# Part of a projection's row sums moved from TensorE to VectorE in the first stage of a transformer block

## The chip, the cores and the metric

The kernel runs on one core of a Trainium2 chip. The metric is the device time of one execution in microseconds (us). All data are float32 in memory. Engines: TensorE (PE; PEld is its weight load), VectorE (DVE), ScalarE (ACT), GpSimd (POOL), and SyncE (SP), which issues most of the transfers (DMA).

## The reference, cut to what matters

The whole block computes a modulated norm, two attention branches, a gated projection, and a feed-forward part with a convolution. The change touches only the first lines:

```python
c_act = jax.nn.silu(c)                       # 1 x 1024
mod = c_act @ w_ada[l] + b_ada[l]            # 1 x 6144
sh_m, sc_m, gt_m, sh_f, sc_f, gt_f = jnp.split(mod, 6, axis=-1)
h = modulate(rms_norm(x, g_mix[l]), sh_m, sc_m)   # 256 x 1024
proj = jnp.einsum('bsd,de->bse', h, w_in[l])      # its first 1536 columns: qa, ka, va
```

Feature `d` of `h` needs `sh_m[d]` and `sc_m[d]`, so it needs column `d` and column `1024 + d` of `c_act @ w_ada`: sums over 1024 rows.

## The kernel before, in words

The first stage works through the 1024 features in eight tiles `j` of 128. For each tile it loads `ada{j}` (two 1024 x 128 column strips of `w_ada`, laid out as 128 partitions x 2 x 8 row blocks x 128) and `wA{j}` (128 rows of `w_in`, 1536 columns). `row_sums(j)` forms the 256 column sums: for each of the eight row blocks `k` one product with the stationary operand `cw[:, k, :]`, which is 32 columns wide and holds `c` in column 0 and zeros elsewhere. Block `k` goes to the column group `k % 4` of the array, so two blocks are accumulated in each of the four groups of one PSUM bank, `cs`. VectorE copies `cs` to `row` (line 460). `column_sums(j)` (line 466) adds up the partitions of `row` and turns the sums into columns, `h`. From those ScalarE makes the scale and shift `ab` (lines 507 and 508) and the modulated features in rounded form, `hh` (line 509); VectorE makes the remainder `hl` (lines 514 and 515).

A product with a weight is formed from three: `hh` with the rounded weight `wh`, `hl` with `wh`, and `hh` with the weight's remainder `wl`. For the weight rows of a tile, `wh` comes from ScalarE in two pieces, `whA` and `whB` (line 553), and `wl` from VectorE in two, `wlA` and `wlB` (line 556). `products(j)` are the 30 products of tile `j`: 24 into the accumulators `pA` (line 472) and six into `pV` (line 477).

The order in this stage is written by hand, and each engine runs its list from front to back. In the loop over `j`, TensorE runs the first `M1[j]` products of tile `j` (9, 7, 5, and then 4), the row sums of tile `j + 1`, nine more products of tile `j`, the column sums of tile `j + 1`, and then the rest of tile `j`. VectorE runs, for tile `j + 1`: `row`, `wlA`, `hf` and `hl`, `wlB`. The loads of `wA{j+3}` and `ada{j+4}` follow at the end of an iteration. There are four buffers for `ada`, three for the raw weights.

After tile 7 come the gate projections (`ps_ga`, line 329) and the rest of the block, with TensorE busy almost without a break.

Of the kernel before, what the change touches and what calls it, by code (L numbers as in the profile page):

```python
# [9 lines left out]
F32 = mybir.dt.float32  # L10
F32R = mybir.dt.float32r
AF = mybir.ActivationFunctionType
ALU = mybir.AluOpType
# [4 lines left out]
P = 128  # L18
D = 1024
KT = D // P  # L20
S = 256
# [32 lines left out]
def block_kernel(ctx: ExitStack, tc: tile.TileContext, x, c, w_ada, b_ada, g_mix, w_in, w_br_moba,  # L54
                 w_br_sb, w_out, rel_bias, g_ffn, w_up, w_conv, b_conv, w_down, g_final, out):
    nc = tc.nc
# [5 lines left out]
    start = ExitStack()  # L62
    start.enter_context(tc.manual_schedule())
    const = ctx.enter_context(tc.tile_pool(name="const", bufs=1))
# [4 lines left out]
    small = ctx.enter_context(tc.tile_pool(name="small", bufs=2))  # L69
# [9 lines left out]
    def bank(pool, name):  # L79
        return pool.tile([P, 512], F32, tag="bank", name=name)  # L80
# [21 lines left out]
    ca = const.tile([P, KT], F32, name="ca")  # L102
# [9 lines left out]
    cw = const.tile([P, KT, 32], F32, name="cw")  # L112
    nc.vector.memset(cw, 0.0)
    nc.vector.tensor_copy(cw[:, :, 0], ca)


    warm = bank(sm, "warm")
# [228 lines left out]
    def tick():  # L346
        for task in list(tasks):
            task[0] -= 1
            if task[0] < 0:
                try:  # L350
                    task[0] = (next(task[1]) or 1) - 1
                except StopIteration:
                    tasks.remove(task)
# [70 lines left out]
    def bias_load():  # L424
        nc.sync.dma_start(toep, bass.AP(tensor=rdram.tensor, offset=rdram.offset,
                                          ap=[[1, P], [512, NH], [1, S]]))
# [11 lines left out]
    ads, wws = {}, {}  # L438

    def ada_load(j):  # L440

        ads[j] = st.tile([P, 2, KT, P], F32, tag="ada", name=f"ada{j}", bufs=4)
        for i in range(2):
            c0 = i * D + j * P
            nc.sync.dma_start(ads[j][:, i, :, :], w_ada[:, c0:c0 + P].rearrange("(k p) f -> p k f", p=P))

    def win_load(j):
        wws[j] = raw_tile(f"wA{j}")
        nc.sync.dma_start(wws[j][:, :1536], w_in[j * P:(j + 1) * P, QA:QA + 1536])  # L449

    def row_sums(j):


        cs = bank(sm, f"cs_{j}")
        for k in range(KT):
            g = slice(k % 4 * 32, k % 4 * 32 + 32)
            nc.tensor.matmul(cs[g, 0:S].rearrange("p (i f) -> p i f", i=2), cw[:, k, :], ads[j][:, :, k, :],  # L457
                             start=k < 4, stop=k >= 4)
        row = small.tile([P, S], F32, tag="acc0", name=f"row_{j}")
        nc.vector.tensor_copy(row, cs[:, 0:S])  # L460
        return row

    def column_sums(j, row):
        ps = bank(sm, f"h1_{j}")
        for i in range(2):
            nc.tensor.matmul(ps[:, i:i + 1], row[:, i * P:(i + 1) * P], ones[:, 0:1], start=i == 0, stop=i == 1)
        return ps

    def products(j, wp):

        def qk(n, f):
            nc.tensor.matmul(psqk[f // 2][:, f % 2 * S:(f % 2 + 1) * S], wp[0][n == 2][:, f * P:(f + 1) * P],  # L472
                             (hh, hl, hh)[n][:, j, :], start=j == 0 and n == 0 and f % 2 == 0,
                             stop=j == KT - 1 and n == 2 and f % 2 == 1)

        def v(n, t):
            nc.tensor.matmul(psv[t], (hh, hl, hh)[n][:, j, t * P:(t + 1) * P], wp[1][n == 2][:, 0:512],  # L477
                             start=j == 0 and n == 0, stop=j == KT - 1 and n == 2)

        if j == KT - 1:  # L480
            for b in (0, 2, 1, 3):
                for n in range(3):
                    for f in (2 * b, 2 * b + 1):
                        qk(n, f)
                        yield
            for t in range(NT):
                for n in range(3):
                    v(n, t)
                    yield
            return  # L490
        for n in range(3):
            for f in range(KT):
                qk(n, f)
                yield
            for t in range(NT):
                v(n, t)
                yield

    def run(gen, n=None):
        while n is None or n > 0:  # L500
            if next(gen, gen) is gen:
                return
            n = None if n is None else n - 1

    def modulated(j, ps):
        ab = small.tile([P, 2], F32, tag="ab", name=f"ab_{j}")
        nc.scalar.activation(ab[:, 0:1], ps[:, 1:2], AF.Identity, bias=bg[:, j:j + 1], scale=gmix[:, j:j + 1])
        nc.scalar.activation(ab[:, 1:2], ps[:, 0:1], AF.Identity, bias=vc[:, j:j + 1])
        nc.scalar.activation(hh[:, j, :], xT[:, j, :], AF.Identity, bias=ab[:, 1:2], scale=ab[:, 0:1])
        return ab  # L510

    def h_lo(j, ab):
        hf = small.tile([P, 512], F32, tag="hf", name=f"hf_{j}", bufs=3)[:, :S]
        nc.vector.tensor_scalar(hf, xT[:, j, :], ab[:, 0:1], ab[:, 1:2], op0=ALU.mult, op1=ALU.add)
        nc.vector.tensor_sub(hl[:, j, :], hf, hh[:, j, :].bitcast(F32))
# [22 lines left out]
    bg = const.tile([P, KT], F32, name="bg")  # L538
    nc.vector.tensor_mul(bg, b1[:, 8:16], gmix)
    row = row_sums(0)  # L540
    warm_up(4)
    put_xT(1, xt[1], nc.vector.tensor_copy)
# [3 lines left out]
    def w_parts(j):  # L546


        wh = [whp.tile([P, 1024], F32R, tag="wh", name=f"wh{x_}{j}") for x_ in "AB"]
        wl = [wlp.tile([P, 1024], F32R, tag="wl", name=f"wl{x_}{j}") for x_ in "AB"]  # L550

        def hi(i, a, n):
            nc.scalar.copy(wh[i][:, a:a + n], wws[j][:, i * 1024 + a:i * 1024 + a + n])  # L553

        def lo(i, a, n):
            nc.vector.tensor_sub(wl[i][:, a:a + n], wws[j][:, i * 1024 + a:i * 1024 + a + n],  # L556
                                 wh[i][:, a:a + n].bitcast(F32))

        return list(zip(wh, wl)), hi, lo
# [13 lines left out]
    for j in range(KT):  # L573
        todo = products(j, wp)
        if j + 1 < KT:
            wp, hi, lo = w_parts(j + 1)
            run(todo, M1[j])
            row = row_sums(j + 1)
            run(todo, M2)
            hi(0, 0, 1024)  # L580
            ab = modulated(j + 1, column_sums(j + 1, row))
            hi(1, 0, 512)
            lo(0, 0, 1024)
            h_lo(j + 1, ab)
            lo(1, 0, 512)
        run(todo)
        if j + 3 < KT:
            win_load(j + 3)
        if j + 4 < KT:
            ada_load(j + 4)  # L590
        if j == 4:
            bias_load()
        if j == 3:
            nc.scalar.copy(onesr, ones)
            nc.scalar.copy(tri, trif)
        tick()
# [581 lines left out]
```

## Time and profile before

| | us |
|---|---|
| median of three runs (lowest, highest) | 420.02 (418.63, 420.79) |
| the profiled execution's own time | 418.87 |
| its span, first to last instruction | 417.1 |
| TensorE busy / VectorE busy in the span | 402.3 / 315.8 |
| ScalarE busy / GpSimd busy in the span | 253.9 / 25.9 |

The profile is one execution. A row of a timeline gives the start and the length in us, engine, source line, operation, what is written from what, and how many instructions were merged into the row; brackets give the idle time before it and what ended that. On TensorE the length of a row includes the pipeline's end, so the start of the next row says when the engine went on. A row of the chain of waits gives start and length of a piece of the work that ended last.

### The profile page before, as it was taken

The page shows a single profiled execution, that of the slowest core. Times are in us where ns is not written, and L with a number is a line of the kernel's source. Part 1 is how long each engine was busy: PE and PEld are TensorE (multiplying, and loading weights), DVE is VectorE, ACT ScalarE, POOL GpSimd, SP SyncE. Part 2 cuts the span into 40 slices and gives each one's busy share as a digit, 9 for nine tenths or more (in the row PEclk, how much of TensorE's full clock was granted, in tenths as well). Part 3 has the DMA queues.
Part 4 walks back from the last instruction along what each step waited for, and adds up shares of the span by engine and source line. Part 5 has one row for each costly group of instructions (what it writes and reads, how often), then busy time and mean ns, then how long its engine had stood idle before and what let it go on. Part 6 is the DMA issues. An engine that isn't in the chain of part 4 may idle for free.

```text
span 417.1 us, 7453 instructions
## 1 busy us (share of the span) xinstructions
PE 402.3 (96%) x2956; PEld 369.1 (88%) x2956; DVE 315.8 (76%) x474; ACT 253.9 (61%) x405; POOL 25.9 (6%) x64
## 2 busy tenths in 40 slices
PE   7999999999999999999979999999999999999992
PEld 6778899999999999999857999999999998888881
DVE  3645579788578979999597899999978888546433
ACT  4544477787697897816375658666766676343412
POOL 4500000000000110000330000000000000000000
PEclk9999999999999999999999999999999999999997
DMA  8999998977556875876957686877566555564002
GB/s 272 335 327 332 341 323 272 334 253 258 198 179 229 262 281 173 281 239 224 321 167 240 211 263 215 264 243 250 166 212 182 202 170 170 176 242 133 21 0 101
DMA packets 75082, 94.49 MB, mean 227 GB/s; under 512 B 2573, under 2 KB 61072, under 8 KB 75047
## 3 DMA queue, kind: packets, MB, share of 16 engines
q1 hardware_dynamic: 74135, 91.82, 68.2%
q10 hardware_dynamic: 576, 1.57, 1.0%
q0 software_dynamic: 336, 0.62, 0.4%
q8 instruction: 23, 0.38, 0.4%
q14 instruction: 12, 0.10, 0.1%
HBM read 92.94 MB, written 1.06 MB: 225 GB/s over the span
## 4 chain that ended last, share of the span: by engine, by line
PE 88%; SPq 3%; DMA 3%; DVE 3%; issue 1%; ACT 1%; POOL 0%; POOLq 0%; ACTq 0%
PE ps_up L298 27%; PE ps_down L185 15%; PE ps_ga L329 6%; PE ps_gb L329 6%; PE pA L472 4%; PE ps_out L185 4%; PE ps_vb L329 3%; PE ps_qb L329 3%; PE ps_yb L329 3%; PE ps_kb L329 3%; PE ps_ya L329 3%; DMA ada<-in_w_ada_dram 2%; PE ps_up L185 2%; PE pV L477 2%; SPq L449 2%; PE cs L457 1%
## 5 line engine op out<-in xcount | busy, mean ns | idle before, releaser
L143 ACT CAST wh_up<-raw_up 128x1024 fp32r<-128x1024 f32 x44 | 46.1, 1049 | 26.6 <-PE ps_up L298 21.5
L298 PE MATMUL ps_up<-h2h__2633,wh_up 128*128 128x256 f32 x320 | 57.7, 282 | 0.0
L298 PE MATMUL ps_up<-h2h__2633,wl_up 128*128 128x256 f32 x320 | 57.4, 281 | 0.0
L298 PE MATMUL ps_up<-h2l__2634,wh_up 128*128 128x256 f32 x320 | 57.4, 281 | 0.0
L148 DVE TENSOR_TENSOR wl_up<-raw_up,wh_up 128x1024 fp32r<-128x1024 f32 x42 | 50.9, 1220 | 7.0 <-ACT wh_up L143 6.9
L298 PEld LDWEIGHTS ps_up<-h2h__2633,wh_up 128*128 128x128 f32 x320 | 46.4, 188 | 0.2
L298 PEld LDWEIGHTS ps_up<-h2h__2633,wl_up 128*128 128x128 f32 x320 | 46.3, 188 | 0.0
L298 PEld LDWEIGHTS ps_up<-h2l__2634,wh_up 128*128 128x128 f32 x320 | 46.3, 188 | 0.0
L148 DVE TENSOR_TENSOR wl_down<-raw_down,wh_down 128x1024 fp32r<-128x1024 f32 x22 | 26.9, 1224 | 25.5 <-ACT wh_down L143 25.5
L143 ACT CAST wh_down<-raw_down 128x1024 fp32r<-128x1024 f32 x22 | 23.1, 1052 | 32.1 <-PE ps_down L185 23.6
L1040 DVE SCALAR_TENSOR_TENSOR cv<-ps_up,wc,cv 128x255 f32<-128x255 f32 (+1 forms) x80 | 34.6, 477 | 1.4 <-ACT cv L1034 0.8
L185 PE MATMUL ps_down<-wh_down,hl_a 128*128 128x512 f32 x88 | 34.8, 395 | 0.0
L185 PE MATMUL ps_down<-wl_down,hh_a 128*128 128x512 f32 x88 | 34.8, 395 | 0.0
L185 PE MATMUL ps_down<-wh_down,hh_a 128*128 128x512 f32 x88 | 34.8, 395 | 0.0
L1034 ACT ACTIVATE cv<-ps_up,vc,wc 128x256 f32<-128x256 f32 x40 | 20.4, 561 | 5.9 <-PE ps_up L298 5.9
L553 ACT CAST whA<-raw_wA 128x1024 fp32r<-128x1024 f32 (+1 forms) x9 | 8.6, 952 | 21.3 <-DMA raw_wA<-in_w_in_dram 21.3
L185 PEld LDWEIGHTS ps_down<-wh_down,hl_a 128*128 128x128 f32 x88 | 16.5, 188 | 4.0
L185 PEld LDWEIGHTS ps_down<-wh_down,hh_a 128*128 128x128 f32 x88 | 16.6, 188 | 3.9
L185 PEld LDWEIGHTS ps_down<-wl_down,hh_a 128*128 128x128 f32 x88 | 16.5, 188 | 3.9
L556 DVE TENSOR_TENSOR wlA<-raw_wA,whA 128x1024 fp32r<-128x1024 f32 x8 | 9.8, 1226 | 8.5 <-ACT whA L553 8.4
L329 PE MATMUL ps_gb<-hh,wh_gb 128*128 128x256 f32 x64 | 13.2, 288 | 0.0
L329 PE MATMUL ps_ga<-hh,wh_ga 128*128 128x256 f32 x64 | 13.2, 288 | 0.0
(280 smaller groups left out, 968.6 us busy)
## 6 DMA issues: line engine op xcount, KB each, us to landing
raw_up<-in_w_up_dram SPq DMA_DIRECT2D x44, 512.0 KB, 5.3
raw_down<-in_w_down_dram SPq DMA_DIRECT2D x10, 1024.0 KB, 4.9
ada<-in_w_ada_dram SPq DMA_DIRECT2D x16, 512.0 KB, 8.1
raw_wA<-in_w_in_dram SPq DMA_DIRECT2D x8, 768.0 KB, 9.4
raw_ga<-in_w_in_dram SPq DMA_DIRECT2D x4, 1024.0 KB, 9.8
ada_gtm<-in_w_ada_dram SPq DMA_DIRECT2D x8, 512.0 KB, 5.4
ada_shf<-in_w_ada_dram SPq DMA_DIRECT2D x8, 512.0 KB, 5.0
raw_gb<-in_w_in_dram SPq DMA_DIRECT2D x4, 1024.0 KB
```

What stands on the lines that cost most here:

```text
L143: nc.scalar.copy(wh, t[:, a:a + 1024])
L148: eng.tensor_sub(wl, t[:, a:a + 1024], wh.bitcast(F32))
L185: nc.tensor.matmul(ps, sx(k)[:, sl], w[:, c0:c0 + n], start=first and i == 0, stop=last and i == 2)
L298: nc.tensor.matmul(st.ps[f // 2][:, f % 2 * S:(f % 2 + 1) * S], wi[:, kk * 512 + f * P:kk * 512 + (f + 1) * P], sx(k0 + kk), start=first a ...
L329: nc.tensor.matmul(st.ps[:, f * S:(f + 1) * S], cols[:, a] if st.fm else x_[:, a], x_ if st.fm else cols, start=first and kk == n == f == ...
L449: nc.sync.dma_start(wws[j][:, :1536], w_in[j * P:(j + 1) * P, QA:QA + 1536])
L472: nc.tensor.matmul(psqk[f // 2][:, f % 2 * S:(f % 2 + 1) * S], wp[0][n == 2][:, f * P:(f + 1) * P], (hh, hl, hh)[n][:, j, :], start=j == 0 ...
L477: nc.tensor.matmul(psv[t], (hh, hl, hh)[n][:, j, t * P:(t + 1) * P], wp[1][n == 2][:, 0:512], start=j == 0 and n == 0, stop=j == KT - 1 an ...
L553: nc.scalar.copy(wh[i][:, a:a + n], wws[j][:, i * 1024 + a:i * 1024 + a + n])
L556: nc.vector.tensor_sub(wl[i][:, a:a + n], wws[j][:, i * 1024 + a:i * 1024 + a + n], wh[i][:, a:a + n].bitcast(F32))
L1034: nc.scalar.activation(ct[:, b, :], tp[:, b * S:(b + 1) * S], AF.Identity, bias=bconv[:, fb:fb + 1], scale=wc[:, 88 + fb:89 + fb])
L1040: nc.vector.scalar_tensor_tensor(ct[:, b, d:], tp[:, b * S:(b + 1) * S - d], wc[:, (2 - d) * 44 + fb:(2 - d) * 44 + fb + 1], ct[:, b, d:], ...
```

## The change

For feature tiles 4 to 7, row blocks 3 to 7 of the weighted sum are formed on VectorE: one operation multiplies block 3 by `c`, and four more each multiply a block by `c` and add it to the sum so far, `csum`. They are in VectorE's list right after `wlB` of the tile before, one iteration ahead of the row sums that use them. TensorE then forms four products instead of eight: blocks 0, 1 and 2 as before, and `csum` with `ow`, which holds a one in column 0 and zeros elsewhere. Each of the four goes to its own column group. Tiles 0 to 3 are as before.

```diff
+    ow = const.tile([P, 32], F32, name="ow")
+    nc.vector.memset(ow, 0.0)
+    nc.vector.memset(ow[:, 0:1], 1.0)
+    sums = {}
...
         cs = bank(sm, f"cs_{j}")
-        for k in range(KT):
+        ops = [(cw[:, k, :], ads[j][:, :, k, :]) for k in range(KT)]
+        if j in sums:
+            ops[3:] = [(ow, sums[j])]
+        for k, (c_, a_) in enumerate(ops):
             g = slice(k % 4 * 32, k % 4 * 32 + 32)
-            nc.tensor.matmul(cs[g, 0:S].rearrange("p (i f) -> p i f", i=2), cw[:, k, :], ads[j][:, :, k, :],
-                             start=k < 4, stop=k >= 4)
+            nc.tensor.matmul(cs[g, 0:S].rearrange("p (i f) -> p i f", i=2), c_, a_, start=k < 4,
+                             stop=k + 4 >= len(ops))
...
+    def sum_rows(j):
+
+        sums[j] = (small.tile([P, 512], F32, tag="hf", name=f"csum_{j}", bufs=3)[:, 0:S]
+                   .rearrange("p (i f) -> p i f", i=2))
+        for k in range(3, KT):
+            if k == 3:
+                nc.vector.tensor_scalar(sums[j], ads[j][:, :, k, :], ca[:, k:k + 1], None, op0=ALU.mult)
+            else:
+                nc.vector.scalar_tensor_tensor(sums[j], ads[j][:, :, k, :], ca[:, k:k + 1], sums[j], op0=ALU.mult,
+                                               op1=ALU.add)
+            yield
...
             lo(1, 0, 512)
+            if 4 <= j + 2 < KT:
+                run(sum_rows(j + 2))
         run(todo)
```

In VectorE's list before, around the row copy of tile 4 (`row_501`; `wlB_423` belongs to tile 3, `wlA_486` to tile 4):

```order
L514 TENSOR_SCALAR hf_459<-xT,ab_453 128x256 [waits Activation_49]
L515 TENSOR_TENSOR hl<-hf_459,hh 128x256 [waits DVE_49,Activation_49]
L556 TENSOR_TENSOR wlB_423<-raw_wA_351,whB_357 128x512 [waits Activation_49]
L460 COPY row_501<-cs_492 128x256 [waits PE_49]
L556 TENSOR_TENSOR wlA_486<-raw_wA_415,whA_484 128x1024 [waits DMAHW5_49,Activation_49]
```

The same place in VectorE's list now (`row_506` is the row copy of tile 4, `csum_466` its partial sum):

```order
L533 TENSOR_SCALAR hf_462<-xT,ab_456 128x256 [waits Activation_49]
L534 TENSOR_TENSOR hl<-hf_462,hh 128x256 [waits DVE_49,Activation_49]
L575 TENSOR_TENSOR wlB_426<-raw_wA_354,whB_424 128x512 [waits Activation_49]
L476 TENSOR_SCALAR csum_466<-ada_356,ca 128x256 [waits DMAHW4_49,DMAHW3_49]
L478 SCALAR_TENSOR_TENSOR csum_466<-ada_356,ca,csum_466 128x256 [waits DVE_49] x4
L467 COPY row_506<-cs_501 128x256 [waits PE_49]
L575 TENSOR_TENSOR wlA_495<-raw_wA_418,whA_493 128x1024 [waits DMAHW5_49,Activation_49]
```

Five operations stand between `wlB` of tile 3 and the row copy of tile 4; the first waits for the load of `ada4`, each of the other four for the one ahead of it.

In TensorE's list before, around the row sums of tile 4 (`cs_492`), with the first products of tile 3 ahead of them:

```order
L472 MATMUL pA_267<-hh,whA_420 128x256 [waits Activation_49]
L472 MATMUL pA_267<-hh,whA_420 128x256
L472 MATMUL pA_268<-hh,whA_420 128x256 x2
L457 MATMUL cs_492<-ada_353,cw 32x256 [waits DMAHW4_49,DMAHW3_49,PE_49]
L457 MATMUL cs_492<-ada_353,cw 32x256 x7
L472 MATMUL pA_269<-hh,whA_420 128x256 x2
```

The same place in TensorE's list now (`cs_501` are the row sums of tile 4):

```order
L491 MATMUL pA_270<-hh,whA_423 128x256 [waits Activation_49]
L491 MATMUL pA_270<-hh,whA_423 128x256
L491 MATMUL pA_271<-hh,whA_423 128x256 x2
L464 MATMUL cs_501<-ada_356,cw 32x256 [waits DMAHW4_49,DMAHW3_49,PE_49]
L464 MATMUL cs_501<-ada_356,cw 32x256 x2
L464 MATMUL cs_501<-csum_466,ow 32x256 [waits DVE_49]
L491 MATMUL pA_272<-hh,whA_423 128x256 x2
```

The row sums stand where they stood, after four products of tile 3. Four of the eight are gone, and the last one left waits for VectorE.

## Rows read from the trace of the kernel before

**Rows 1.** The page's first part: busy us (share of span) and instructions of each engine.

```profile
PE 402.3 (96%) x2956; PEld 369.1 (88%) x2956; DVE 315.8 (76%) x474; ACT 253.9 (61%) x405; POOL 25.9 (6%) x64
```

**Rows 2.** The chain of waits, around and after the stage: start us, us, what.

```profile
17.59 9.49 DMA ada<-in_w_ada_dram
27.22 1.07 PE cs L457 x16
...
58.91 1.40 PE pV L477 x6
60.31 4.37 PE ps_ga L329 x36
```

**Rows 3.** Windows, one tile: PE, PEld, DVE, ACT, POOL busy; clock, DMA, GB/s.

```profile
38.00:43.88 5.88, 5.88 (x51) 4.90 (x51) 3.27 (x6) 2.67 (x5) 0.55 (x1) 1.00 1.13 330
```

**Rows 4.** Timeline of TensorE: row sums of tile 4; products and column sums of tile 5.

```profile
32.97 1.07 PE L457 MATMUL cs<-ada,cw 128*32 128x256 f32 x16
...
39.85 0.75 PE L472 MATMUL pA<-hh,whA 128*128 128x256 f32 x4
...
41.24 0.50 PE L466 MATMUL h<-ones,row 128*128 128x1 f32 x4
```

**Rows 5.** Short timelines of TensorE inside the row sums of tile 6.

```profile
44.72 0.42 PE L457 MATMUL cs<-ada,cw 128*32 128x256 f32 x4
44.96 0.61 PE L457 MATMUL cs<-ada,cw 128*32 128x256 f32 x8
45.17 0.61 PE L457 MATMUL cs<-ada,cw 128*32 128x256 f32 x8
45.39 0.40 PE L457 MATMUL cs<-ada,cw 128*32 128x256 f32 x4
45.72 0.39 PE L472 MATMUL pA<-hh,whA 128*128 128x256 f32 x1
```

**Rows 6.** Timeline of VectorE: end of tile 3; tile 5 to the next row copy.

```profile
32.24 0.69 DVE L556 TENSOR_TENSOR wlB<-raw_wA,whB 128x512 fp32r<-128x512 f32 x1
...
42.32 0.41 DVE L514 TENSOR_SCALAR hf<-xT,ab 128x256 f32<-128x256 f32 x1
...
43.46 0.69 DVE L556 TENSOR_TENSOR wlB<-raw_wA,whB 128x512 fp32r<-128x512 f32 x1
45.86 0.42 DVE L460 COPY row<-cs 128x256 f32<-128x256 f32 x1 [1.70 <-PE cs L457]
```

**Rows 7.** Timeline of ScalarE, tile 5.

```profile
41.78 0.35 ACT L507 ACTIVATE ab<-h,bg,vc 128x1 f32<-128x1 f32 x1 [0.65 <-PE h L466]
...
42.32 0.60 ACT L509 ACTIVATE hh<-xT,ab 128x256 fp32r<-128x256 f32 x1
```

**Rows 8.** VectorE's multiply-and-adds: durations by line (min/median/max ns), and one run.

```profile
L1040 DVE SCALAR_TENSOR_TENSOR cv<-ps_up,wc,cv x80: 466/475/486, 244.2 to 351.9; 128x255 f32<-128x255 f32 x40, 128x254 f32<-128x254 f32 x40
L839 DVE SCALAR_TENSOR_TENSOR acc_gtm<-ada_gtm,ca,acc_gtm x8: 1275/1280/1285, 71.0 to 104.8; 128x1024 f32<-128x1024 f32 x8
279.78 2.81 DVE L1040 SCALAR_TENSOR_TENSOR cv<-ps_up,wc,cv 128x255 f32<-128x255 f32 x7
```

**Rows 9.** Timeline of VectorE at the start.

```profile
3.86 0.27 DVE L113 MEMSET cw<- 128x256 f32 x1
4.17 0.17 DVE L114 COPY cw<-ca 128x8 f32<-128x8 f32 x1
5.41 0.15 DVE L133 TENSOR_SCALAR ms_n<-ss 128x1 f32<-128x1 f32 x1 [1.07 <-ACT sq L390]
```

**Rows 10.** Waits, one of TensorE: us in total, times, longest us.

```profile
PE ps_up L185 <- ACT h2h__2633 L153: 2.3, 1, 2.3
```

**Rows 11.** Windows, the stretch that holds this wait; columns as in rows 3.

```profile
206.00:228.00 22.00, 18.84 (x88) 14.26 (x87) 17.41 (x30) 13.51 (x25) 7.05 (x5) 1.00 0.63 198
```

**Rows 12.** One load of ada for tile 5: issue times, and us to landing.

```profile
L445 SPq DMA_DIRECT2D ada<-in_w_ada_dram x1: 1630/1630/1630, 29.4 to 29.4; - x1
DMA to landing us min/median/max: 8.7/8.7/8.7
```

## Prediction

> **What bounds the kernel now.** I read the page's busy times first. TensorE is busy for 96% of the span, VectorE for 76% [rows 1], so anything taken from TensorE counts if nothing else is made late. Then the chain of waits. Until 27 us it runs through transfers: the load of tile 3's `ada` is the last thing waited for, and from the row sums behind it the chain stays on TensorE, through tiles 3 to 7 and on into the gate projections [rows 2]. Tiles 4 to 7 are thus the part of the stage that TensorE alone sets. The windows, cut from tile to tile, show it: in the 5.88 us of one tile TensorE is busy for all of it, VectorE for 3.27 [rows 3]. Read as a share, VectorE has 2.6 us free per tile, and the added work would seem to fit. Whether it does hangs on where that free time lies, which only the timelines tell. VectorE idles for 1.70 us just ahead of the row copy [rows 6], and that idle time ends with the row sums, so most of it falls after the moment at which TensorE begins them. Work put there is free only if nobody asks for its result before the row sums are over. The last of the new row sums does ask.
>
> **What is removed.** The sixteen instructions of one tile's row sums (two for each float32 product) start in four rounds of four, at 44.72, 44.96, 45.17 and 45.39, and the next product begins at 45.72 [rows 5]: 1.00 us in all, each round some 0.22, the last 0.33 up to the next product. Two products per column group take four rounds, so one per group takes two. Without any wait a tile's row sums would last 0.57 us in place of 1.00. That saves 0.43 us a tile, and over four tiles 1.7 us.
>
> **What is added.** Five VectorE operations per tile on 256 columns. The trace has no such operation on `ada`; the nearest are the multiply-and-add on 255 columns, 0.475 us, and `hf`, a multiply on 256 columns, 0.41 us [rows 6, 8]. From below, seven such multiply-and-adds in one run took 2.81 us, one every 0.39, so they overlap a little; five in that rhythm end 2.04 us after the first starts. But those lie interleaved with operations on other tiles, while the new ones form a chain in which each waits for the one ahead. For such a wait the nearest row is `cw`: a fill of 0.27 us at 3.86, and the copy into it begins at 4.17, 0.04 after its end [rows 9]. With that, the chain takes 0.41 + 0.04 + 3 x (0.475 + 0.04) + 0.475 = 2.47 us. From above I allow 0.69 us each, what `wlB` costs on twice the columns [rows 6]: 3.45. I take 2.47, since it is built from rows of nearly the same size.
>
> The Trainium skill ("VectorE: DVE Perf Modes", section "The DRAIN you can't avoid") says that a semaphore behind each of a run of chained operations costs nothing over a single one at the end. By it the chain would take 2.04 us and not 2.47; the `cw` row speaks mildly against it, and what it would make of the time stands among the rivals.
>
> **Where the chain lies: the first tile.** VectorE starts `wlB` of tile 3 at 32.24, for 0.69 us [rows 6]; the next operation can start about 0.08 before its end (the overlap of the run of seven), at 32.85. The load it needs is there, since TensorE began the same tile's row sums at 32.97 with no idle time before them [rows 4]. So TensorE arrives when the chain has just begun. It ends at 35.32. I add 0.04 for the hand-over and then the last product: its two instructions sit in one column group and take two rounds, 0.22 + 0.33 = 0.55. TensorE goes on at 35.91, where before it went on at 32.97 + 1.00 = 33.97. Loss: 1.94 us, the saving of that tile included. Everything behind stands in the same queue: the other 26 products of tile 3, the column sums of tile 4, and so all of tile 4.
>
> **The three tiles after it.** A late start alone would move everything once. But the next chain hangs on this one through a loop. From the moment at which TensorE goes on after the row sums (39.85 for tile 5 in the trace): nine products up to the column sums at 41.24, so 1.39 [rows 4]; `ab` at 41.78, 0.54 later, having waited for TensorE; `hh` and `hf` at 42.32, another 0.54 [rows 6, 7]; `wlB` at 43.46, 1.14 later; the chain could start at 44.07, 0.61 later. Up to here 4.22 us. Then 2.47 for the chain, 0.04, and 0.55 for the last product: 7.28 us. TensorE's own round in the kernel before is 5.87, from 39.85 to 45.72 [rows 4, 5]. VectorE and TensorE now wait for each other in turn, and each of tiles 5, 6 and 7 takes 1.41 us longer: 4.23. The loads don't add to this: the second load of tile 5's `ada`, issued at 29.4, lands 8.7 later at 38.1 [rows 12], and the chain for tile 5 can't begin before 35.91 + 4.22 = 40.1.
>
> **The small parts.** The two fills of `ow` fall into the 1.07 us for which VectorE waits for ScalarE near the start [rows 9]; uncovered they would cost no more than `cw`'s 0.27 each. The load queue issues the same transfers in the same order, those that wait for `wlB` a little later, and at 60.31 TensorE enters work that, in the chain, no load holds up [rows 2]. `csum` shares its three buffers with `hf`; the user of each is two iterations old when its buffer comes round.
>
> **Sum.** 1.94 + 4.23 = 6.2 us later at the end of tile 7's row sums. Behind that TensorE has no idle time that could take it back, so it reaches the end. Against the profiled execution's own 418.87 us (span 417.1 and 1.8 around it) that is 425.0; against the median of the three runs, 420.02, it is 426.2. I give 425.5, between the two.
>
> **Rivals.**
> *The chain is as short as its operations in a run.* At 2.04 us a tile loses 0.43 less: 1.51 + 3 x 0.98 = 4.5, or 423.3 on the profiled time. If the last product's two instructions also take one round (tail 0.33), it is 0.22 less per tile: 3.6, or 422.4. For it: the 0.39 rhythm. Against it: no two neighbours in that run depend on each other.
> *Only the first tile loses.* If the later chains had the time, because `wlB` were set by loads and not by TensorE, TensorE would lose 1.94 once and save 0.43 three times: +0.65, or 419.5. Against it: `ab` waited 0.65 us for TensorE's column sums [rows 7], which ties `wlB` to TensorE.
> *The sums are early enough (the other side).* The loop turns even when 4.22 + chain + 0.04 + 0.55 falls to 5.87, at a chain of 1.06 us, and gives all of the 1.7 us at 0.63: 417.2 at best. That needs some 0.2 us per operation. In its favour is proportion: 1024 columns take 1.28 us [rows 8], a quarter of it 0.32. But even 0.32 is too much, and the 255-column row shows 0.475.
> *The clock falls.* TensorE will idle for about 2.0 us in tile 4 and 1.4 in each of the next three. If its granted clock went to the lower of its two levels (1.2 in place of 2.4 GHz) after each, a tile's matmuls would take up to twice as long: up to 5 us a tile, 20 in all, 445. Against it: an idle time of 2.3 us passes in a window whose clock is 1.00 [rows 10, 11]. [...]
>
> **Chances.** The forecast 63% (its own range 423.5 to 428; with operations of 0.69 us it would be 0.98 more per tile, 429.0), the short chain 20%, the first tile alone 7%, early sums 5%, the clock 5%. What measurement of this kernel can't tell from no change is about 0.5%, 2.1 us: slower than that are the first two and the clock, and a short chain has a little over it, 0.86 with a part of the short chain's low end taken off; within it the first-tile case and that part, 0.10; faster 0.04, as even the best case of early sums is only just over the bound. The range, 421.8 to 428.0, leaves out the clock, early sums, the first-tile case and a little of the forecast's upper end.
>
> **What would show it.** In the profile after: in tiles 4 to 7 the last row-sums product idles until the fifth sum on VectorE, some 2 us and then 1.4 each; tile to tile 7.3 us and not 5.87; VectorE's run of five about 2.5 us; the idle time ahead of its row copy gone; the clock at 1.00. The forecast is wrong if the five take under 1.1 us together, if `wlB` of a tile doesn't move with TensorE's column sums, or if the gate projections start less than 3 us later than at 60.31.

## The result, and the profile after

The changed kernel took 426.28 us (median; 424.65 to 427.88), the kernel before 419.42 in the same comparison: a ratio of 1.0164, 95% interval 1.0141 to 1.0188. The forecast was 425.5 us, with a range of 421.8 to 428.0. The profiled execution has a span of 425.7 us against 417.1, 8.6 more.

First the page of the changed kernel, its busy times and the granted clock in 40 slices of the span (9 is full, a digit is a tenth):

```profile
PE 406.5 (95%) x2924; PEld 372.1 (87%) x2924; DVE 325.3 (76%) x496; ACT 253.4 (60%) x405; POOL 25.8 (6%) x64
...
PEclk9996999999999999999998999999999999999998
```

TensorE issues 32 matmuls fewer than before [rows 1] and is still busy 4 us longer. The clock row shows where most of that comes from: a 6 in the fourth slice (32 to 43 us). The timeline of TensorE shows where the span grew; line 464 is the row sums, 485 the column sums, 491 the first products after them:

```profile
33.16 0.63 PE L464 MATMUL cs<-ada,cw 128*32 128x256 f32 x6
35.60 0.66 PE L464 MATMUL cs<-csum,ow 128*32 128x256 f32 x2 [1.81 <-DVE csum L478]
36.18 1.22 PE L491 MATMUL pA<-hh,whA 128*128 128x256 f32 x4
...
44.08 0.63 PE L464 MATMUL cs<-ada,cw 128*32 128x256 f32 x6
44.47 0.62 PE L464 MATMUL cs<-csum,ow 128*32 128x256 f32 x2
45.02 0.75 PE L491 MATMUL pA<-hh,whA 128*128 128x256 f32 x4
...
51.73 0.62 PE L464 MATMUL cs<-csum,ow 128*32 128x256 f32 x2 [1.21 <-DVE csum L478]
52.28 0.74 PE L491 MATMUL pA<-hh,whA 128*128 128x256 f32 x4
...
58.98 0.62 PE L464 MATMUL cs<-csum,ow 128*32 128x256 f32 x2 [1.22 <-DVE csum L478]
59.53 0.74 PE L491 MATMUL pA<-hh,whA 128*128 128x256 f32 x4
```

Read the starts of line 491 against each other. From the start of tile 4's row sums to the next product it is 3.02 us, where before it was 1.00 [rows 4, 5]. Then tile to tile: 8.84, 7.26 and 7.25 us, where before it was 5.87. VectorE's timeline has the reason on the other side:

```profile
32.51 0.69 DVE L575 TENSOR_TENSOR wlB<-raw_wA,whB 128x512 fp32r<-128x512 f32 x1
33.11 0.35 DVE L476 TENSOR_SCALAR csum<-ada,ca 128x256 f32<-128x256 f32 x1
33.50 2.04 DVE L478 SCALAR_TENSOR_TENSOR csum<-ada,ca,csum 128x256 f32<-128x256 f32 x4
36.29 0.43 DVE L467 COPY row<-cs 128x256 f32<-128x256 f32 x1 [0.75 <-PE cs L464]
...
47.49 0.41 DVE L533 TENSOR_SCALAR hf<-xT,ab 128x256 f32<-128x256 f32 x1 [0.81 <-ACT ab L527]
48.13 0.42 DVE L534 TENSOR_TENSOR hl<-hf,hh 128x256 fp32r<-128x256 f32 x1 [0.22 <-ACT hh L528]
48.64 0.69 DVE L575 TENSOR_TENSOR wlB<-raw_wA,whB 128x512 fp32r<-128x512 f32 x1
49.25 0.35 DVE L476 TENSOR_SCALAR csum<-ada,ca 128x256 f32<-128x256 f32 x1
49.63 2.05 DVE L478 SCALAR_TENSOR_TENSOR csum<-ada,ca,csum 128x256 f32<-128x256 f32 x4
```

The chain of five ends 2.43 us after it begins, and TensorE goes on 0.64 us behind its end (35.54 to 36.18). Ahead of the chain, VectorE waits for ScalarE's `ab`, and ScalarE's timeline shows that `ab` waits for TensorE's column sums `h`; so TensorE and VectorE take turns:

```profile
46.96 0.35 ACT L526 ACTIVATE ab<-h,bg,vc 128x1 f32<-128x1 f32 x1 [4.38 <-PE h L485]
```

The chain of waits names the same pieces and the start of the gate projections:

```profile
58.44 0.50 DVE csum L478
58.94 0.04 issue
58.98 0.62 PE cs L464 x2
...
68.24 4.36 PE ps_ga L333 x36
```

Gate projections start 7.93 us later than before [rows 2]. This is the sum of 0.18 (the stage came to tile 4 that much later, at the wait for tile 3's load), 2.02 in tile 4, and then 2.97, 1.39 and 1.38. Of the 2.97, some 1.58 are more than the next two tiles show; the windows, tile to tile, say what is different there (the last three columns are granted clock, DMA share, GB/s):

```profile
36.18:45.02 8.84, 8.84 (x43) 7.57 (x43) 5.20 (x10) 2.96 (x7) 0.55 (x1) 0.62 1.10 344
45.02:52.28 7.26, 6.05 (x43) 4.77 (x42) 5.29 (x10) 2.56 (x5) 0.00 (x0) 1.00 1.10 339
52.28:59.53 7.25, 6.03 (x43) 4.75 (x42) 5.29 (x10) 2.56 (x5) 0.00 (x0) 1.00 0.78 246
```

Behind the first wait the clock stood at 0.50, the lower level of 1.2 GHz, from about 36.1 to 42.9 us. TensorE came so late to tile 5's row sums that the chain was nearly done and no wait is left there: part of what the clock cost was taken off the wait. Up to the norm the 7.93 us shrink to 7.55 (its first product behind the wait starts at 226.68, before at 219.13). A second low stretch, from about 227.2 to 230.6 us, behind the norm's wait of 2.28 us, brings them to the 8.6 of the whole span; the kernel before has that wait too [rows 10].

### The profile page after: what moved, and what is told of

It is laid out like the page before. It is cut to its first block, busy times and chain, and to the rows that moved or that the text cites. A ratio compares the mean times of both kernels' runs of the same rounds, so it can differ in the third digit from the quotient of the medians.

```text
span 425.7 us, 7416 instructions
## 1 busy us (share of the span) xinstructions
PE 406.5 (95%) x2924; PEld 372.1 (87%) x2924; DVE 325.3 (76%) x496; ACT 253.4 (60%) x405; POOL 25.8 (6%) x64
## 3 DMA queue, kind: packets, MB, share of 16 engines
q10 hardware_dynamic: 576, 1.57, 1.0%
## 4 chain that ended last, share of the span: by engine, by line
PE 87%; DVE 4%; DMA 3%; issue 2%; ACT 2%; POOL 0%; POOLq 0%; ACTq 0%; DVEq 0%
PE ps_up L302 27%; PE ps_down L189 14%; PE ps_ga L333 6%; PE ps_gb L333 5%; PE pA L491 4%; PE ps_out L189 4%; PE ps_up L189 3%; PE ps_vb L333 3%; PE ps_qb L333 3%; PE ps_yb L333 3%; PE ps_kb L333 3%; PE ps_ya L333 3%; DMA raw_wA<-in_w_in_dram 2%; PE pV L496 2%; DVE csum L478 1%
## 5 line engine op out<-in xcount | busy, mean ns | idle before, releaser
L526 ACT ACTIVATE ab<-h,bg,vc 128x1 f32<-128x1 f32 x8 | 2.8, 349 | 17.6 <-PE h L485 17.5
```

## The experiments

Theory: TensorE waits for a chain that is built too late, and from then on a loop (column sums, `ab`, `hh`, `hl`, `wlB`, the five sums, last product) sets the tile. A lowered clock comes on top in some executions. Rivals are named with each. All times are medians beside the kernel before on the same chip; its medians were 419.75 (for the first four runs), 419.95 (the next three) and 419.80 (the last two).

**The changed kernel again.**

> The changed kernel itself once more. Theory (a loop of TensorE and VectorE costs 6 us, and in some executions a lowered clock behind the first stall costs 2 to 3 us more): the times fall into two groups, near 424.9 and near 427.5, and the profile's granted clock in tile 4 goes with its own time. Rival (the loop alone, 7 us, the clock row is chance): one group around 426.3 whatever the clock.

Measured: 426.61 us, ratio 1.0166 (1.0145 to 1.0186). Its profile repeats the first: a wait of 1.83 us in tile 4, then a clock of 0.50, tiles of 8.84, 7.27 and 7.25. The two groups did not show: these four times, 426.03 to 427.18, make one group, as the rival has it, and none lies near 424.9. With the mean granted clock of each execution beside its time, the eight executions of both runs are: 0.995 425.16, 0.994 424.65; 0.992 426.21, 0.991 426.03; 0.988 427.01, 0.987 427.88; 0.983 427.18 and 427.40. The two profiled executions are those at 0.983, with both low stretches. So the time goes with the clock, roughly, from 425 to 427.9, and the two executions with the highest mean clock, 424.65 and 425.16, lie at the 425.0 of the forecast's sum. Which stretch the others had is inferred from the mean, not seen. Part of it is not the change's: executions of the kernel before also lie near 418.9 at 0.995 and near 420.0 at 0.991 or 0.992.

**TensorE's part alone** (blocks 4 to 7 are left out of the sums).

```diff
-            ops[3:] = [(ow, sums[j])]
+            ops[4:] = []
...
-                run(sum_rows(j + 2))
+                sums[j + 2] = None
```

> TensorE's part of the change alone: for tiles 4 to 7 only row blocks 0 to 3 are summed, four products in place of eight, no sums on VectorE (blocks 4 to 7 are left out of the result). Theory: each tile saves 0.43 us, and TensorE then arrives at tile 7's row sums just about when its load lands: 1.3 to 1.7 us faster than before, about 417.9. Rival (the stage is paced by its loads already): within 0.5 us of before.

Measured: 418.98 us, ratio 0.9982 (0.9969 to 0.9996): 0.8 us faster (between 0.2 and 1.3), half of the 1.7 that four products a tile are worth. TensorE's timeline, and the row of the kernel before that goes with the last one:

```profile
32.97 0.64 PE L464 MATMUL cs<-ada,cw 128*32 128x256 f32 x8
...
38.98 0.64 PE L464 MATMUL cs<-ada,cw 128*32 128x256 f32 x8 [0.52 <-DMA ada<-in_w_ada_dram]
39.55 0.74 PE L491 MATMUL pA<-hh,whA 128*128 128x256 f32 x4
...
44.92 0.64 PE L464 MATMUL cs<-ada,cw 128*32 128x256 f32 x8 [0.45 <-DMA ada<-in_w_ada_dram]
...
60.39 0.51 PE L333 MATMUL ps_ga<-hh,wl_ga 128*128 128x256 f32 x2 [0.52 <-DVE wl_ga L152]
```

```profile
60.38 0.50 PE L329 MATMUL ps_ga<-hh,wl_ga 128*128 128x256 f32 x2
```

The freed time turns into waits for the loads of `ada`, and at the end for the first gate weights. In this profile nothing of the gain is left there (60.39, before 60.38); about 0.4 us come up only between there and the norm (218.77, before 219.13), so where the 0.8 us of the medians arise is not shown. Even free of charge, the sums could have brought about 0.2%. The result lies between theory and rival, and nearer to the rival than expected.

**VectorE's part alone** (the sums are formed and not used).

```diff
-        if j in sums:
-            ops[3:] = [(ow, sums[j])]
```

> VectorE's part alone: the five sums are formed as in the change, but nobody reads them; TensorE forms all eight products. Theory (what costs is that TensorE's last product waits for the sums, and the loop that this closes): VectorE's own round is about 5.8 us, under TensorE's 5.87, so only the first tile is late: at most 0.6 us slower than before, about 419.9. Rival (VectorE is simply overloaded and delays row copies and remainders): 3 us slower or more, 422.5 or above.

Measured: 420.32 us, ratio 1.0012 (0.9998 to 1.0026), within the 0.6 us that the theory allowed. The same twenty operations stand in VectorE's list:

```profile
38.75 0.35 DVE L474 TENSOR_SCALAR csum<-ada,ca 128x256 f32<-128x256 f32 x1
39.13 2.05 DVE L476 SCALAR_TENSOR_TENSOR csum<-ada,ca,csum 128x256 f32<-128x256 f32 x4
41.10 0.42 DVE L465 COPY row<-cs 128x256 f32<-128x256 f32 x1
```

The row copy now waits for VectorE itself and no longer for TensorE, and its result is just in time; only in tile 4 do the column sums start 0.27 us later than before (35.64 against 35.37). VectorE's load is not the loss; that TensorE's last product reads the sums is.

**The wait filled with dummy products.**

```diff
+            if len(ops) == 4 and k == 3:
+                for _ in range(8 if j == 4 else 5):
+                    nc.tensor.matmul(cs[:, S:S + P], ones, ident, start=True, stop=True)
             g = slice(k % 4 * 32, k % 4 * 32 + 32)
```

> The change, with dummy products (128 columns, into unused columns of the same bank) just ahead of the product that waits: eight in tile 4, five in tiles 5 to 7, so that TensorE is busy while it would wait. Theory (the clock falls because of the first idle stretch): granted clock 1.00 through tiles 4 to 7, no group of times near 427.5, all near 424.9, so about 1.4 us under the changed kernel's median; tile to tile still 7.25 us. Rival (the low clock has nothing to do with the idle time, or costs nothing as the wait hides it): the same times as the changed kernel.

Measured: 426.23 us (425.99 to 427.07), ratio 1.0160 (1.0140 to 1.0180). Windows, tile to tile, columns as above:

```profile
36.42:43.80 7.38, 7.36 (x53) 5.96 (x52) 5.20 (x10) 3.06 (x7) 0.55 (x1) 1.00 1.08 340
43.80:51.10 7.30, 7.30 (x53) 5.96 (x52) 5.29 (x10) 2.57 (x5) 0.00 (x0) 1.00 1.09 339
```

With TensorE kept busy, the clock of this profile stays at 1.00 behind tile 4's dummies, and that tile takes 7.38 us and not 8.84. The loop stays: idle time itself is not what costs 7.3. The expected time, 424.9, was missed by 1.3 us, and the total is the rival's, that of the changed kernel: three of the four executions still show a mean clock of 0.991 or 0.992 (the profiled one has its low stretch at the norm), and filling makes the round 0.05 longer. The lower clock means of 0.983 to 0.988 did not occur. The fourth execution took 427.07 at 0.995, which this account does not explain.

**The sums earlier in VectorE's list.**

```diff
             lo(0, 0, 1024)
+            if 4 <= j + 2 < KT:
+                run(sum_rows(j + 2))
             h_lo(j + 1, ab)
             lo(1, 0, 512)
-            if 4 <= j + 2 < KT:
-                run(sum_rows(j + 2))
```

> The change with the five sums placed earlier in VectorE's list: behind wlA and ahead of hf, hl and wlB, instead of behind wlB. All else is as in the change. Theory (the loss is the loop from TensorE's column sums through hh, hl and wlB to the sums): the sums no longer hang on TensorE, only on the load of ada, which lands at 38.1, 43.7 and 49.2 for tiles 5 to 7; with 2.4 us of sums and 0.6 of the last product TensorE goes on at about 41.1, 46.7 and 52.2, 0.6 us later than before at the end of tile 7; a lowered clock behind the wait in tile 4 may add up to 1.3: 420.0 to 421.3, some 5 us under the changed kernel. Rival (five more operations a tile are too much for VectorE wherever they stand): 425 or above.

Measured: 420.73 us, ratio 1.0019 (1.0007 to 1.0032), 5.9 us under the changed kernel's 426.61, with the same operations. VectorE's timeline:

```profile
32.66 0.35 DVE L476 TENSOR_SCALAR csum<-ada,ca 128x256 f32<-128x256 f32 x1 [1.13 <-DMA ada<-in_w_ada_dram]
...
38.31 0.35 DVE L476 TENSOR_SCALAR csum<-ada,ca 128x256 f32<-128x256 f32 x1 [0.30 <-DMA ada<-in_w_ada_dram]
38.76 2.04 DVE L478 SCALAR_TENSOR_TENSOR csum<-ada,ca,csum 128x256 f32<-128x256 f32 x4
...
49.78 0.35 DVE L476 TENSOR_SCALAR csum<-ada,ca 128x256 f32<-128x256 f32 x1 [0.63 <-DMA ada<-in_w_ada_dram]
```

In three of the four tiles the chain now starts when `ada` lands (in tile 6, at 43.79, right behind `wlA`), not when TensorE's column sums have gone round. TensorE has one listed wait for the sums, 1.57 us in tile 4, and the clock stays at 1.00 there. What is left, 0.8 us, goes with the load, which lands too late for a chain of 2.4 us to be over when TensorE asks.

**The column sums sooner.**

```diff
-            run(todo, M2)
+            run(todo, 4 if j >= 3 else M2)
```

> The change with TensorE's column sums five products sooner behind the row sums (four products between them instead of nine) for tiles 4 to 7. Theory (the loop sets tile to tile): one link of the loop goes from 1.39 to about 0.65 us, so tiles 6 and 7 take 6.5 us in place of 7.25, and the whole about 2.2 us less than the changed kernel, near 424.2. Rival (VectorE's amount of work or the loads set the tile): tile to tile stays at 7.25 and the time at 426.5.

Measured: 423.91 us, ratio 1.0093 (1.0074 to 1.0112). TensorE's timeline:

```profile
42.50 0.62 PE L464 MATMUL cs<-csum,ow 128*32 128x256 f32 x2 [0.49 <-DVE csum L478]
...
49.05 0.62 PE L464 MATMUL cs<-csum,ow 128*32 128x256 f32 x2 [0.36 <-DVE csum L478]
...
55.60 0.62 PE L464 MATMUL cs<-csum,ow 128*32 128x256 f32 x2 [0.40 <-DVE csum L478]
```

Tile to tile it is 6.55 us, against a worked-out 6.5. Shortening a link on TensorE, with nothing taken from VectorE, shortens the tile by what the link lost: the loop is shown.

**Tile 4 alone.**

```diff
-            if 4 <= j + 2 < KT:
+            if j + 2 == 4:
```

> The change for tile 4 alone; tiles 5 to 7 are summed by TensorE as before. Theory (first tile 2.0 us, each later tile 1.4 by the loop, and the lowered clock behind the first wait 1 to 2): 2.0 us over before with the clock at 1.00 and up to 3.6 with the low clock in tile 4, so 421.5 to 423.2; tiles 5 to 7 again 5.87 apart at full clock. Rival (nearly all of the loss is made in the first tile and its clock): 425 or above. Rival (later tiles take the loss back): 419.8.

Measured: 421.84 us, ratio 1.0045 (1.0027 to 1.0062), 1.9 us. TensorE's timeline:

```profile
35.31 0.62 PE L464 MATMUL cs<-csum,ow 128*32 128x256 f32 x2 [1.66 <-DVE csum L478]
...
40.72 1.07 PE L464 MATMUL cs<-ada,cw 128*32 128x256 f32 x16
...
46.60 1.07 PE L464 MATMUL cs<-ada,cw 128*32 128x256 f32 x16
```

The first tile costs its 2 us and nothing is taken back: later tiles are 5.88 and 5.87 us apart again. The clock stayed at 1.00 behind this wait of 1.66 us.

**The loads exchanged**, with sums right behind the row copy; and the exchange alone, in the kernel before.

```diff
-        if j + 3 < KT:
-            win_load(j + 3)
         if j + 4 < KT:
             ada_load(j + 4)
+        if j + 3 < KT:
+            win_load(j + 3)
```

> The change with the sums still earlier in VectorE's list (right behind the row copy, ahead of wlA) and with the load of ada for four tiles on issued ahead of that of wA for three tiles on, instead of behind it. Theory (what is left of the loss with early sums is that ada lands only 0.6 to 1.4 us before TensorE wants it): ada then lands some 2.4 us sooner, TensorE no longer waits for sums, and each of tiles 4 to 7 saves 0.43 us; wA for tile 3 lands some 3 us later and costs TensorE 0.9 us once: about 1 us faster than before, 418.9 (418.2 to 420.2). Rival (the loads as a whole set the stage, their order doesn't matter): 420.7, as with early sums alone. A faster version than both kernels is possible only under the theory.

> The kernel before with only the order of these loads exchanged, no sums on VectorE: what the exchange costs or gives by itself. Theory: 0.9 us slower than before, 420.8, since the waits for wA of tile 3 are paid and nothing is saved. Rival (order of loads doesn't matter): 419.9.

Measured: 421.61 us, ratio 1.0064 (1.0034 to 1.0094), and for the exchange alone 423.26, ratio 1.0098 (1.0067 to 1.0129). TensorE in the first of the two:

```profile
34.83 0.73 PE L491 MATMUL pA<-hh,whA 128*128 128x256 f32 x4 [2.26 <-ACT hh L528]
...
40.96 0.42 PE L464 MATMUL cs<-ada,cw 128*32 128x256 f32 x3
...
46.40 0.42 PE L464 MATMUL cs<-ada,cw 128*32 128x256 f32 x3
```

Both miss what was expected, 418.9 and 420.8. Between the two kernels lie 1.6 us, but their intervals overlap, and in the profile of the exchange alone the clock stood at 0.50 from about 34.7 to 38.1 us, behind the same wait; its rows there are longer than at full clock (0.73 and 1.07 us):

```profile
34.77 1.22 PE L472 MATMUL pA<-hh,whA 128*128 128x256 f32 x4 [2.19 <-ACT hh L509]
35.93 1.94 PE L457 MATMUL cs<-ada,cw 128*32 128x256 f32 x16
```

So the medians alone show no gain by the sums. The trace of the first kernel does: its tiles are 5.47, 5.44 and 5.66 us apart, where before it was 5.87, so with `ada` early and the chain outside the loop products are saved. But the exchange costs 2.2 us in tile 3 and not 0.9: ScalarE's list has the late `whA` ahead of `ab` and `hh`, which I had left out, and times spread up to 425.7 at mean clocks down to 0.980. No version that computes the whole result beats the kernel before; one that also reorders ScalarE's list for tile 3 wasn't tried.

## Why the prediction was right, point by point

- *What bounds the stage.* Right: the wait that replaced the saved products is on TensorE's own path, and everything behind moved with it (7.93 us at the gate projections, 7.55 at the norm; the four-products kernel gains 0.4 us over that part as well, so this is not the change's).
- *The saving, 1.7 us.* Too high as a best case: 0.8 in the medians without any sums, and nothing by the gate projections of that profile, since `ada` and then the gate weights come no sooner. The early-sums rival's 417.2 was not reached even so (lowest of twelve: 417.90).
- *The chain, 2.47 us.* 2.43. The multiply takes 0.35 and not 0.41; the four that follow start 0.52 apart, 0.13 more than in an independent run [rows 8]. The rival built on 2.04 us falls with it. The independent run also differs in its operands (a PSUM tile, 255 columns); whether they or the waits make the 0.13 us was not tried. The Trainium skill ("VectorE: DVE Perf Modes", section "The DRAIN you can't avoid") found no cost of semaphores in a run of eight copies. This chain does not bear that out, nor does it settle it.
- *First tile, 1.94 us.* 2.02 in the profile; with tile 4 alone the whole kernel lost 1.9.
- *The loop, 7.28 us per tile.* 7.26 and 7.25 where the clock is full, and 6.55 with a shorter link.
- *The loads don't add to this.* Right for the change as it stands; with the sums early they are the limit (chain starts at 32.66, 38.31 and 49.78, each ended by a landing).
- *The clock, 5%.* Misjudged, and left out of the range. I took one idle time of 2.3 us at full clock [rows 10, 11] for proof that shorter ones are harmless. The first wait, 1.81 and 1.83 us in two profiles, was followed by some 6.8 us at the lower level, which added 1.6 us to that tile's round, while waits of 1.57, 1.66 and 1.74 in the profiles of three other kernels were not. The filled kernel, where the wait is gone and the clock stays, points to idle time as the condition; as the clock also stayed behind some waits, one profile does not prove it. The Trainium skill ("TensorE: Matmul & The Clock Gate", section "Why this matters for your kernels") warns of idle gaps between bursts of matmuls, but of longer ones than these 1.81 and 1.83 us; here the measurement decides. The priced loss, up to 5 us in every tile, was far too high: only one wait of four had it, and slow matmuls ran where TensorE would have waited.
- *Where the median stands.* The sum's 6.2 us fit the executions with the highest mean clock (424.65 and 425.16, against 425.0 on the profiled time); the measured 6.9 holds the low clock of some others. That the median still came out 0.8 us from the forecast is in part luck: the low clock, at which one execution took 427.88, was not in the sum.
- *The signs named.* Most came true: tile to tile 7.25, the run of five 2.43 us, TensorE's waits 1.81 and 1.2. Two did not: the clock fell, and VectorE still idles 0.71 to 0.75 us ahead of its row copy, for it now waits through TensorE's last product.

## What to carry to other kernels

Idle time of an engine counts only where it lies: VectorE's 2.6 us free per tile were worth nothing, because the new work stood between another engine's result and the next thing that engine asked for. Before moving work, walk the loop once around through all engines and add up its links; if the sum passes the tile's time, every tile pays the difference. And ask when the work's input lands: work done a step ahead needs its data a step sooner.

## What the runs showed of the hardware

- The same idle time of TensorE, about 2.28 us at the norm, was followed by a clock of 1.00 in three profiled executions (the kernel before and both with loads exchanged) and of 0.50 for some 3.4 us in the other eight. In tile 3 a wait of 2.26 us (loads exchanged, with sums) was followed by 1.00 and one of 2.19 (the exchange alone) by 0.50. The length of a wait alone does not tell. In the windows of the changed kernel's profile:

```profile
226.00:227.00 1.00, 0.32 (x1) 0.30 (x2) 0.91 (x3) 1.00 (x3) 0.17 (x1) 1.00 0.96 293
228.00:229.00 1.00, 1.00 (x4) 0.81 (x3) 1.00 (x3) 0.00 (x0) 0.26 (x1) 0.50 1.06 383
```

- A float32 product into one 32-column group takes two rounds, one for each of its instructions, however few groups are in use: the last product alone took TensorE 0.55 us to get past (51.73 to 52.28, at full clock), four at once 0.57 (38.98 to 39.55 in the four-products kernel).
